# Decoder step on one core: cached latent pages pre-turned by numpy and loaded page by page from SyncE

## The chip, the cores and the metric

The kernel runs on one core of a Trainium2 chip. The metric is device time in microseconds (us) for one launch; runs of one kernel on the same inputs are compared, and the median is quoted. Engines are named as in the profile: PE (TensorE matmul), DVE (VectorE), ACT (ScalarE), POOL (GpSimd), SP (SyncE, which here only issues DMAs).

## The reference, cut to what matters

One inference step of a two-layer trunk: a Mamba-2 SSD layer, then a multi-head latent attention (MLA) layer, for a prompt of 1024 tokens and for 8 sample sequences of 8 new tokens each. The change touches only the sample part of the MLA layer, where the queries attend to 2048 cached tokens per sequence, held in pages of 128 tokens. A page has a latent part (128 x 256) and a rotary part (128 x 32), and `page_table` (8 x 16) says where in the pool each page lies:

```
s = (q_lat . ckv[page_table] + q_pe . kpe[page_table]) * MLA_SCALE      # 128 query rows per sequence
m, l, acc: running maximum, sum of exp, and exp(s - m) @ ckv[page_table]
```

So every latent page is used twice: as keys, with the 256 latent columns on the partitions, and as values, with the tokens on the partitions.

## The kernel before, in words

All matrix products are made of float32 operands split into a high and a low part (`split`: ACT casts the high part, DVE or POOL subtracts for the low part), so one product is three matmuls. The program runs the SSD layer, the MLA projections and gate blocks (about 1010 to 1240 us), sixteen prompt heads (to about 1655), and then the sample attention with the output projection woven into it (1632 to 1915).

The sample attention is the generator `Sample.flow`. It walks over 32 **items**, four for each sequence; an item is four pages, 512 tokens. The order of PE and POOL is as written there (`manual_schedule`); the order of ACT, DVE and SP comes from the framework's scheduler, and each engine runs its own list strictly in order. In step n of the flow:

- `turn(n+1, 0)` and `turn(n+1, 1)` turn the raw page rows of the next item with eight PE transposes (tiles `ct`, four to a PSUM bank) and `split` each bank into `cTh`, `cTl`.
- `turn_p(n-1)` turns the weights of the item before (tile `pt`), which becomes `pTh`, `pTl`.
- `scores(n)` is seven matmuls of 512 columns (tile `sc`); `weigh(n)` is the maximum on DVE and the exp on ACT.
- pieces of the output projection (tile `p`, line 101, twelve matmuls a piece) fill PE, one or two pieces a step from step 9 on. Their result `h` leaves through SP (`out_y_prompt`, line 2016).
- `values(n-1)` is twelve matmuls (tile `o`); `halves(n+1)` splits the raw rows of the next item into `kvh` (ACT) and `kvl` (POOL, four subtractions).
- `load(n+4)` fetches an item: one indirect DMA on POOL's queue, 128 partitions with four token rows of 1 KB each, at addresses from the index tile `ptidx`. Four buffers `pgr` hold raw items (`PRE = 4`). `load_tk` fetches the turned rotary keys of two items at a time, in three DMAs on SP.

The rotary cache is prepared earlier, among the gate blocks: `gather_kpe` collects all 128 rotary pages with one indirect DMA (`kprows`), turns them with 32 PE transposes (`kpt`), splits them (`kpeh`, `kpel`) and writes both to DRAM (`kpe_d`). `page_rows` works out `ptidx` on DVE.

Of the kernel before, what the change touches and what calls it, by code (L numbers as in the profile page):

```python
# [46 lines left out]
SB = {"tr": 4, "sc4": 2, "on": 1, "pj": 1}  # L47
QG = 2
PRE = 4
# [1134 lines left out]
class Heads:  # L1184
# [152 lines left out]
    def load_q(self, pr):  # L1337
        k, nc = self.k, self.k.nc
        qt = self.sp.tile([128, 9, 192], F32, tag="qp", name=f"qp{pr}", bufs=2 if pr else 1)
# [152 lines left out]
def mla_heads(k, hd, sm, early, st):  # L1492
# [46 lines left out]
def gather_kpe(k, pool):  # L1539
    nc, I = k.nc, k.I  # L1540
    idx = pool.tile([128, 1], mybir.dt.int32, name="kpidx")
    nc.sync.dma_start(idx, I["page_table"].rearrange("b (p o) -> (b p) o", o=1))
    rows = pool.tile([NB * NPG, PAGE * ROPE], F32, name="kprows")
    nc.gpsimd.indirect_dma_start(rows, None, I["cache_kpe"].rearrange("o n t c -> (o n) (t c)"),
                                 bass.IndirectOffsetOnAxis(idx, 0), bounds_check=k.npool - 1)
    kh = pool.tile([128, NB * NPG, 32], F32R, name="kpeh")
    kl = pool.tile([128, NB * NPG, 32], F32R, name="kpel")
    rv = rows.rearrange("g (s x) -> g s x", s=32)
    yield
    for g in range(8):  # L1550
        p = k.psum.tile([128, 512], F32, tag="tr", name=f"kpt{g}", bufs=PB["tr"])
        for j in range(4):
            nc.tensor.transpose(p[:, 128 * j : 128 * j + 128], rv[:, 4 * g + j], k.ident)
        split(k, kh[:, :, 4 * g : 4 * g + 4], kl[:, :, 4 * g : 4 * g + 4], p.rearrange("p (s g) -> p g s", s=4))
        yield
    k.kpe_d = []
    for n, t in (("h", kh), ("l", kl)):
        d = k.dram.tile([4, ROPE, NB * NPG * 32], F32, name="kpe_d" + n)
        nc.sync.dma_start(d.rearrange("r c x -> (r c) x"), t.rearrange("p g s -> p (g s)").bitcast(F32))
        k.kpe_d.append(d)  # L1560


def page_rows(k, pool):
    nc, I = k.nc, k.I
    pt = pool.tile([128, NB * NPG], mybir.dt.int32, name="ptab")
    nc.sync.dma_start(pt, I["page_table"].rearrange("b p -> (b p)").partition_broadcast(128))
    ps = pool.tile([128, 1], F32, name="pslot")
    nc.sync.dma_start(ps, I["c_slot"])
    pf = pool.tile([128, 32], F32, name="ptf")
    for j in range(4):  # L1570
        r = slice(32 * j, 32 * j + 32)
        nc.vector.tensor_copy(pf[r], pt[r].rearrange("p (x j) -> p j x", j=4)[:, j])
    nc.vector.tensor_scalar(pf, pf, 32.0, ps, op0=ALU.mult, op1=ALU.add)
    k.ptidx = k.cm.tile([128, 32], mybir.dt.int32, name="ptidx")
    nc.vector.tensor_copy(k.ptidx, pf)


class Sample:
    def __init__(self, k):
        self.k, self.sp = k, None  # L1580
        self.idx = k.ptidx
# [55 lines left out]
    def late_loads(self):  # L1637
        src = self.k.I["mla_w_uv"][0].rearrange("c h v -> c (h v)")
        self.wv = [self.ep.tile([128, D], F32, tag="pgr", name=f"wv4{c}", bufs=4) for c in range(2)]
# [3 lines left out]
    def load_tk(self, n):  # L1643
        k, nc = self.k, self.k.nc
        tk = self.ep.tile([96, 4, 256], F32R, tag="tk", name=f"tk{n}", bufs=2)
        for j in range(3):
            src = k.kpe_d[j % 2][:, :, 128 * n : 128 * n + 256].rearrange("r c x -> c r x")
            with k.tc.issue_after(k.lastq.ins):
                self.lasttk = nc.sync.dma_start(tk[32 * j : 32 * j + 32].bitcast(F32), src)
        for j in range(2):  # L1650
            self.tk[n + j] = tk[:, :, 128 * j : 128 * j + 128]

    def load(self, n):
        k, nc = self.k, self.k.nc
# [61 lines left out]
    def turn(self, n, c):  # L1716
        k, nc, sp = self.k, self.k.nc, self.sp
        raw = self.raw[n]
        pt = self.pt("tr", f"ct{n}_{c}")
        for j in range(4):  # L1720
            nc.tensor.transpose(pt[:, j * 128 : j * 128 + 128], raw[:, j, c * 128 : c * 128 + 128], k.ident)
        th = self.ep.tile([128, 512], F32R, tag=f"cTh{c}", name=f"cTh{n}_{c}", bufs=2)
        tl = self.ep.tile([128, 512], F32R, tag=f"cTl{c}", name=f"cTl{n}_{c}", bufs=2)
        split(k, th, tl, pt)
        self.cT[n, c] = (th, tl)

    def halves(self, n):
        k, nc = self.k, self.k.nc
        raw = self.raw.pop(n)
# [6 lines left out]
    def scores(self, n):  # L1736
# [3 lines left out]
        c0, c1 = self.cT.pop((n, 0)), self.cT.pop((n, 1))  # L1740
        mm3(nc, ps.rearrange("p (r c) -> p r c", r=4), [(x, y if len(y.shape) == 3 else y.rearrange("p (r c) -> p r c", r=4)) for x, y in (
            (k.qlh[:, 0, b], c0[0]), (k.qlh[:, 0, b], c0[1]), (k.qll[:, 0, b], c0[0]),
            (k.qlh[:, 1, b], c1[0]), (k.qlh[:, 1, b], c1[1]), (k.qll[:, 1, b], c1[0]),
            (k.qpr[:, b], self.tk.pop(n)))])
# [67 lines left out]
    def flow(self):  # L1812
        N = len(self.items)
        for n in range(-1, N + 1):
            t, out = n + 1 < N, self.out
            if t:
                self.turn(n + 1, 0)
# [6 lines left out]
            if t:  # L1824
                self.turn(n + 1, 1)
# [16 lines left out]
            if n % 2 == 0 and n + 2 < N:  # L1842
# [283 lines left out]
```

## Time and profile before

| | |
|---|---|
| time, three runs | 1920.44, 1920.27 and 1915.07 us; median 1920.27 |
| profiled execution | span 1915.0 us; no other time is listed for it, and it agrees with the fastest run, 1915.07 |
| busy share of the span | PE 99%, PE weight loads 90%, DVE 63%, ACT 57%, POOL 43% |
| granted PE clock | mean 0.997 of full speed |
| DMA | 212.5 MB, 111 GB/s over the span |
| the 256 transposes `ct` | from 1631.9 to 1870.4 us |
| the 32 transposes `kpt` | from 1069.7 to 1104.5 us |

A busy PE is not PE at its peak, since matmuls overlap in the pipeline. The time that a group of matmuls takes is better read from the distance between starts, or from the chain of work that ended last.

### The profile page before, as it was taken

Reading aid. Unit: us, or ns where it says so; the run is one execution under the profiler, and the core shown is the slowest. Engines: PE = TensorE matmul, PEld = TensorE weight load, DVE = VectorE, ACT = ScalarE, POOL = GpSimd, SP = SyncE. Lnnn points to the kernel's source line nnn. Section 1 sums busy time; section 2 is a strip of 40 time slices with the busy share of each in tenths; the row PEclk is TensorE's granted clock in tenths of the full one; section 3 lists DMA queues with packets and bytes.
Section 4 is the critical chain, followed back from the end, with each engine's and each line's share of the span. In section 5 each row is a group of like instructions: output and inputs, shape, how many; then the busy total and the mean of one; then the engine's idle time right before and its main releaser. Section 6 shows DMA issues by size and latency. Waiting matters only on the chain.

```text
span 1915.0 us, 33672 instructions
## 1 busy us (share of the span) xinstructions
PE 1887.4 (99%) x12023; PEld 1728.1 (90%) x12023; DVE 1208.5 (63%) x2500; ACT 1101.1 (57%) x2528; POOL 823.3 (43%) x1116
## 2 busy tenths in 40 slices
PE   8999999999999999999999999999999999999998
PEld 7999999999999999888788998898888887888887
DVE  5557676757676767765534214566887878666665
ACT  6467666767666666732214323436777777755552
POOL 2447555555655555453004322103443434764551
PEclk9999999999999999999999999999999999999999
DMA  5223323332323232644424662233111112664451
GB/s 165 54 79 91 94 83 94 88 106 83 101 84 99 85 99 78 212 158 175 166 110 133 209 226 75 69 110 95 47 52 41 53 41 58 228 204 142 146 170 37
DMA packets 183967, 212.51 MB, mean 111 GB/s; under 512 B 19148, under 2 KB 147928, under 8 KB 182776
## 3 DMA queue, kind: packets, MB, share of 16 engines
q1 hardware_dynamic: 177304, 185.32, 31.1%
q0 software_dynamic: 6416, 24.91, 3.8%
q8 instruction: 95, 1.56, 0.3%
q14 instruction: 72, 0.59, 0.1%
q10 hardware_dynamic: 80, 0.13, 0.0%
HBM read 151.76 MB, written 58.52 MB: 110 GB/s over the span
## 4 chain that ended last, share of the span: by engine, by line
PE 90%; DMA 3%; DVE 3%; ACT 3%; issue 1%; POOL 0%; SPq 0%; POOLq 0%; DVEq 0%; ACTq 0%
PE pj L89 24%; PE pz L101 8%; PE pq L101 6%; PE pob L101 5%; PE p L101 5%; PE poa L101 4%; PE py L640 3%; PE sc L89 3%; PE o L89 2%; PE sc L1402 2%; PE o L1465 2%; PE o L1467 2%; PE st L1434 2%; PE st L1435 2%; PE st L1436 2%; PE o L1466 2%
## 5 line engine op out<-in xcount | busy, mean ns | idle before, releaser
L89 PE MATMUL pj<-xl,wih 128*128 128x384 f32 (+1 forms) x768 | 255.4, 333 | 0.0
L89 PE MATMUL pj<-xh,wih 128*128 128x384 f32 (+1 forms) x768 | 252.9, 333 | 1.2 <-ACT xh L276 0.8
L89 PE MATMUL pj<-xh,wil 128*128 128x384 f32 (+1 forms) x768 | 252.9, 329 | 0.0
L1448 POOL TENSOR_TENSOR tl<-P,th 128x384 fp32r<-128x384 f32 (+1 forms) x96 | 90.6, 944 | 232.3 <-ACT P L1446 186.6
L528 DVE SCALAR_TENSOR_TENSOR acc<-raw,vec,acc 128x1112 f32<-128x1112 f32 x96 | 141.6, 1476 | 15.3 <-ACT acc L524 14.4
L89 PEld LDWEIGHTS pj<-xh,wih 128*128 128x128 f32 x768 | 143.8, 188 | 2.6 <-ACT xh L276 1.4
L89 PEld LDWEIGHTS pj<-xl,wih 128*128 128x128 f32 x768 | 144.5, 188 | 1.0
L89 PEld LDWEIGHTS pj<-xh,wil 128*128 128x128 f32 x768 | 144.5, 188 | 0.5
L101 PE MATMUL pz<-wih,xh 128*128 128x256 f32 x504 | 143.3, 288 | 1.4 <-ACT z L569 1.4
L101 PE MATMUL pz<-wil,xh 128*128 128x256 f32 (+1 forms) x504 | 139.8, 283 | 0.0
L1445 ACT ACTIVATE th<-st 128x512 fp32r<-128x512 f32 x192 | 94.6, 493 | 66.6 <-PE st L1441 50.9
L101 PE MATMUL pz<-wih,xl 128*128 128x256 f32 x448 | 128.5, 287 | 0.0
L1733 POOL TENSOR_TENSOR kvl<-pgr,kvh 128x256 fp32r<-128x256 f32 x128 | 97.8, 791 | 70.6 <-ACT kvh L1731 70.3
L635 ACT ACTIVATE M<-M,tok 128x128 f32<-128x128 f32 (+1 forms) x288 | 90.4, 386 | 51.4 <-DVE M L631 51.2
L136 DVE TENSOR_TENSOR wil<-wraw,wih 128x512 fp32r<-128x512 f32 x88 | 74.4, 851 | 38.2 <-ACT wih L130 31.7
L101 PEld LDWEIGHTS pz<-wih,xh 128*128 128x128 f32 x504 | 95.9, 190 | 2.3 <-ACT z L569 1.8
L1446 ACT ACTIVATE P<-st 128x512 f32<-128x512 f32 x192 | 93.5, 487 | 0.0
L101 PEld LDWEIGHTS pz<-wil,xh 128*128 128x128 f32 (+1 forms) x504 | 92.8, 184 | 0.1
L101 PE MATMUL p<-w,oh 128*128 128x512 f32 (+3 forms) x304 | 88.8, 386 | 0.6 <-DVE h L1983 0.6
L616 POOL TENSOR_TENSOR xdd<-xsT,tok 128x256 f32<-128x256 f32 x64 | 50.0, 781 | 86.4 <-ACT xsT L602 83.3
L101 PEld LDWEIGHTS pz<-wih,xl 128*128 128x128 f32 x448 | 85.4, 191 | 0.7
L1448 DVE TENSOR_TENSOR tl<-P,th 128x512 fp32r<-128x512 f32 x96 | 72.1, 752 | 18.9 <-ACT P L1446 18.7
(830 smaller groups left out, 6212.5 us busy)
## 6 DMA issues: line engine op xcount, KB each, us to landing
wraw<-in_ssd_w_in SPq DMA_DIRECT2D x92, 256.0 KB
M<-acs_d SPq DMA_DIRECT2D x64, 256.0 KB
s<-in_state_ssm SPq DMA_DIRECT2D x32, 256.0 KB
y_d<-y SPq DMA_DIRECT2D x64, 128.0 KB
out_s_ssm<-s SPq DMA_DIRECT2D x32, 256.0 KB
q_d<-qt SPq DMA_DIRECT2D x32, 192.0 KB
qp<-q_d SPq DMA_DIRECT2D x8, 768.0 KB
wraw<-in_ssd_w_out SPq DMA_DIRECT2D x10, 512.0 KB
```

The costliest lines, as they stand in the source:

```text
L89: nc.tensor.matmul(out, a, b, start=(i == 0), stop=(i == n - 1))
L101: nc.tensor.matmul(o, a, b, start=(j == 0), stop=(j == len(ops) - 1))
L136: return (eng or nc.vector).tensor_tensor(lo, src, hi.bitcast(F32), op=ALU.subtract)
L528: last = nc.vector.scalar_tensor_tensor(acc, raw[:, j : j + n], k.convw[j][:, blk : blk + 1], acc, op0=ALU.mult, op1=ALU.add)
L616: nc.gpsimd.tensor_tensor(v3(xdd), v3(xsT), hb(2), op=ALU.mult)
L635: nc.scalar.activation(M[:m, h, :m], M[:m, h, :m], AF.Exp, bias=tk[:, 0, 4 * g + h : 4 * g + h + 1])
L640: nc.tensor.matmul(py[:m, h * 64 : h * 64 + 64], M[:m, h, :m], xsT[:m, h * 64 : h * 64 + 64], start=True, stop=True)
L1402: nc.tensor.matmul(ps[:, :n], qh[:96, 128 * i : 128 * i + 128], kh[:96, 512 * c : 512 * c + n], start=True, stop=True)
L1445: nc.scalar.activation(th[:, :n], ps[:, :n], AF.Exp, scale=SCALE)
L1446: nc.scalar.activation(P[:, :n], ps[:, :n], AF.Exp, scale=SCALE)
L1448: eng.tensor_tensor(tl[:, :n], P[:, :n], th[:, :n].bitcast(F32), op=ALU.subtract)
L1733: nc.gpsimd.tensor_tensor(rl[:, j], raw[:, j], rh[:, j].bitcast(F32), op=ALU.subtract)
```

## The change

Numpy now builds two arrays on the host. `c_pages` holds for every page 128 rows of 512 numbers: row p is first the 256 latent values of token p, then the two turned halves (latent columns p and 128 + p over the 128 tokens). `c_rope` holds each rotary page already turned. The kernel then does without the transposes `ct` and `kpt`. `load` becomes four plain DMAs on SP, one for each page (256 KB), with the page number read from SBUF into a register; an item is 1 MB in place of 0.5 MB. There are three buffers in place of four. `cast` splits the turned half straight from SBUF: one ACT cast of 1024 columns and two DVE subtractions of 512. `load_tk` fetches one item at a time. The rotary rows are split in SBUF and written to DRAM in runs of 512 bytes. The index arithmetic of `page_rows` is gone. The PSUM banks for turned tiles go from four to three, and those for the output pieces from one to two; the query tiles `qp` move to a pool that is closed at head 14.

```diff
-SB = {"tr": 4, "sc4": 2, "on": 1, "pj": 1}
+SB = {"tr": 3, "sc4": 2, "on": 1, "pj": 2}
-PRE = 4
+PRE = 3
...
-    nc.gpsimd.indirect_dma_start(rows, None, I["cache_kpe"].rearrange("o n t c -> (o n) (t c)"),
-                                 bass.IndirectOffsetOnAxis(idx, 0), bounds_check=k.npool - 1)
+    nc.gpsimd.indirect_dma_start(rows, None, I["c_rope"], bass.IndirectOffsetOnAxis(idx, 0), bounds_check=k.npool - 1)
...
-        p = k.psum.tile([128, 512], F32, tag="tr", name=f"kpt{g}", bufs=PB["tr"])
-        for j in range(4):
-            nc.tensor.transpose(p[:, 128 * j : 128 * j + 128], rv[:, 4 * g + j], k.ident)
-        split(k, kh[:, :, 4 * g : 4 * g + 4], kl[:, :, 4 * g : 4 * g + 4], p.rearrange("p (s g) -> p g s", s=4))
+        c = slice(512 * g, 512 * g + 512)
+        split(k, kh[:, c], kl[:, c], rows[:, c])
...
+            with k.tc.issue_after(k.lastq.ins):
+                self.lasttk = nc.sync.dma_start(tk[32 * j : 32 * j + 32].bitcast(F32),
+                                                k.kpe_d[j % 2][:, 512 * n : 512 * n + 512])
...
-        raw = self.ep.tile([128, 4 * KVL], F32, tag="pgr", name=f"pgr{n}", bufs=4)
-        nc.gpsimd.indirect_dma_start(raw, None, k.I["cache_ckv"].rearrange("o n (s r) c -> (o n s) (r c)", r=4),
-                                     bass.IndirectOffsetOnAxis(self.idx[:, n : n + 1], 0),
-                                     bounds_check=k.npool * 32 - 1)
+        raw = self.ep.tile([128, 4, 512], F32, tag="pgr", name=f"pgr{n}", bufs=PRE)
+        _, pages = nc.values_load_multi_w_load_instructions(
+            k.ptab[0:1, 4 * n : 4 * n + 4], engines=[nc.sync.engine], min_val=0, max_val=k.npool - 1,
+            skip_runtime_bounds_check_because="the DMA that takes the value checks it against the pool's size")
+        for j, pg in enumerate(pages):
+            nc.sync.dma_start(raw[:, j], k.I["c_pages"][bass.ds(pg, 1)].rearrange("o p c -> (o p) c"))
...
-    def turn(self, n, c):
-        k, nc, sp = self.k, self.k.nc, self.sp
-        raw = self.raw[n]
-        pt = self.pt("tr", f"ct{n}_{c}")
-        for j in range(4):
-            nc.tensor.transpose(pt[:, j * 128 : j * 128 + 128], raw[:, j, c * 128 : c * 128 + 128], k.ident)
-        th = self.ep.tile([128, 512], F32R, tag=f"cTh{c}", name=f"cTh{n}_{c}", bufs=2)
-        tl = self.ep.tile([128, 512], F32R, tag=f"cTl{c}", name=f"cTl{n}_{c}", bufs=2)
-        split(k, th, tl, pt)
-        self.cT[n, c] = (th, tl)
+    def cast(self, n):
+        src = self.raw[n][:, :, 256:].rearrange("p g (c t) -> p c g t", c=2)
+        th, tl = (self.ep.tile([128, 2, 4, 128], F32R, tag="cT" + x, name=f"cT{x}{n}", bufs=2) for x in "hl")
+        self.k.nc.scalar.copy(th, src)
+        for c in range(2):
+            self.k.nc.vector.tensor_tensor(tl[:, c], src[:, c], th[:, c].bitcast(F32), op=ALU.subtract)
+        self.cT[n] = [tuple(x[:, c].rearrange("p g t -> p (g t)") for x in (th, tl)) for c in range(2)]
...
-                self.turn(n + 1, 0)
+                self.cast(n + 1)
...
-                self.turn(n + 1, 1)
...
-            if n % 2 == 0 and n + 2 < N:
+            if n >= 0 and n + 2 < N:
                 self.load_tk(n + 2)
```

The first place is PE's list between the values of one item (`o`) and the scores of the next (`sc`), late in the flow. Before:

```order
L89 MATMUL o_22594<-kvh,pTl_22536 128x256
L1721 MATMUL ct_0_22617<-ident,pgr_22369 128x128 [waits DMASW7_49,Activation_49]
L1721 MATMUL ct_0_22617<-ident,pgr_22369 128x128 x3
L1711 MATMUL o46n<-cn_22455,pn_22567 128x256 [waits DMAHW7_49,PE_49]
L1760 MATMUL pt_22630<-ident,P_22560 128x128 [waits PE_49,Activation_49]
L1760 MATMUL pt_22630<-ident,P_22560 128x128 x3
L1721 MATMUL ct_1_22639<-ident,pgr_22369 128x128 [waits DVE_49]
L1721 MATMUL ct_1_22639<-ident,pgr_22369 128x128 x3
L89 MATMUL sc_22648<-cTh_0_22526,qlh 128x512
```

The same place now:

```order
L89 MATMUL o_22925<-kvh,pTl_22866 128x256
L1700 MATMUL o47n<-cn_22775,pn_22888 128x256 [waits DMAHW7_49,Activation_49]
L1745 MATMUL pt_22957<-ident,P_22881 128x128 [waits Activation_49]
L1745 MATMUL pt_22957<-ident,P_22881 128x128 x3
L89 MATMUL sc_22966<-cTh_22855,qlh 128x512
```

The two groups of four transposes are gone; what is left stands in the old order.

The second place is SP's list late in the flow, where an output tile is written (`out_y_prompt`); `[waits ...]` names the engines or DMA semaphores that a row waits for. Before, where the page loads stood on POOL:

```order
L1935 DMA h_21870<-h_d 128x1024 [waits DMAHW0_49]
L1619 DMA cn_22064<-cs_d 8x256 [waits DMAHW1_49,PE_49]
L2016 DMA out_y_prompt<-h_21556 128x512 [waits DMAHW2_49,DVE_49]
L2016 DMA out_y_prompt<-h_21556 128x512 [waits DMAHW3_49,DVE_49]
L1649 DMA tk_21960<-kpe_dh 32x4x256 [waits DMAHW4_49,PE_49]
L1649 DMA tk_21960<-kpe_dl 32x4x256 [waits DMAHW5_49]
L1649 DMA tk_21960<-kpe_dh 32x4x256 [waits DMAHW6_49]
```

Now (`ISA` is an instruction that handles the page number, `TENSOR_LOAD` reads four numbers of `ptab`):

```order
L1637 DMA tk_22517<-kpe_dh 32x512 [waits DMAHW5_49,PE_49]
L2000 DMA out_y_prompt<-h_22134 128x512 [waits DMAHW6_49,DVE_49]
L1637 DMA tk_22517<-kpe_dl 32x512 [waits DMAHW7_49]
L2000 DMA out_y_prompt<-h_22134 128x512 [waits DMAHW0_49,DVE_49]
L1637 DMA tk_22517<-kpe_dh 32x512 [waits DMAHW1_49]
L1643 TENSOR_LOAD ptab
L1647 ISA
L1647 DMA pgr_22503<-in_c_pages 128x512 [waits DMAHW2_49,Activation_49,Pool_49]
L1647 ISA
L1647 DMA pgr_22503<-in_c_pages 128x512 [waits DMAHW3_49]
L1647 ISA
L1647 DMA pgr_22503<-in_c_pages 128x512 [waits DMAHW4_49]
```

A page load now stands behind the output writes, which wait for DVE, and it waits itself for the ACT cast and the POOL subtraction that free its buffer.

The third place is ACT's list among the gate blocks, where the rotary pages are split. Before, spread over five gate blocks, each behind its transposes:

```order
L130 CAST wgh<-wraw 128x1024 [waits DMAHW1_49,Activation_49,Pool_49]
L994 ACTIVATE gt_12864<-pj 128x384 [waits DMAHW3_49,PE_49,Activation_49]
L994 ACTIVATE gt_12864<-pj 128x384 [waits PE_49]
L130 CAST kpeh<-kpt_12943 128x128x4 [waits DVE_49,PE_49]
L130 CAST kpeh<-kpt_12993 128x128x4 [waits PE_49]
L130 CAST kpeh<-kpt_13031 128x128x4 [waits PE_49]
```

Now all eight in one run, ahead of the two gate activations:

```order
L130 CAST wgh<-wraw 128x1024 [waits DMAHW2_49,Activation_49,Pool_49]
L130 CAST kpeh<-kprows 128x512 [waits DMASW2_49,DVE_49]
L130 CAST kpeh<-kprows 128x512 x7
L994 ACTIVATE gt_12854<-pj 128x384 [waits DMAHW2_49,PE_49,Activation_49]
L994 ACTIVATE gt_12854<-pj 128x384 [waits PE_49]
```

The gate activations `gt`, which empty the PSUM tile `pj` for PE, have moved behind the casts.

## Rows read from the trace of the kernel before

**Rows 1.** The page, part 4: the chain that ended last, by engine.

```profile
PE 90%; DMA 3%; DVE 3%; ACT 3%; issue 1%; POOL 0%; SPq 0%; POOLq 0%; DVEq 0%; ACTq 0%
```

**Rows 2.** Windows: busy us by engine, PEclk, DMA share, GB/s.

```profile
1632.00:1700.00 68.00, 64.88 (x392) 55.59 (x391) 44.73 (x92) 48.21 (x105) 46.07 (x55) 0.95 0.75 252
...
1720.00:1840.00 120.00, 120.00 (x716) 103.77 (x716) 78.88 (x175) 65.00 (x141) 63.09 (x77) 1.00 0.49 154
```

**Rows 3.** Chain in order of time, 1741 to 1756: start us, us, what.

```profile
1752.48 0.44 PE ct L1721 x4
1752.92 0.44 PE pt L1760 x4
1753.36 0.44 PE ct L1721 x4
1753.79 1.63 PE sc L89 x7
```

**Rows 4.** Chain: start of the scores of item 7.

```profile
1690.81 1.63 PE sc L89 x7
```

**Rows 5.** Chain: start of the scores of item 31, the last.

```profile
1877.04 1.64 PE sc L89 x7
```

**Rows 6.** PE's timeline at the first rotary transposes.

```profile
1069.83 1.47 PE L1553 MATMUL kpt<-ident,kprows 128*128 128x128 f32 x12
1071.05 0.39 PE L89 MATMUL pj<-hh,wgh 128*128 128x320 f32 x1
```

**Rows 7.** DVE's timeline at 1621.

```profile
1621.05 4.71 DVE L1448 TENSOR_TENSOR tl<-P,th 128x512 fp32r<-128x512 f32 x1
```

**Rows 8.** POOL's timeline at 1618.

```profile
1618.45 1.61 POOL L1656 DMA_INDIRECT pgr<-in_cache_ckv,ptidx  x1 [0.40 <-issue]
```

**Rows 9.** PE's timeline at 1622, with its idle time.

```profile
1622.78 0.50 PE L1467 MATMUL o<-tl,Vh 128*128 128x512 f32 x1 [1.28 <-POOL tl L1448]
...
1625.82 0.50 PE L1467 MATMUL o<-tl,Vh 128*128 128x512 f32 x1 [0.85 <-DVE tl L1448]
```

**Rows 10.** Windows of 5 us, as rows 2.

```profile
1665.00:1670.00 5.00, 4.37 (x25) 3.06 (x23) 3.27 (x6) 4.09 (x11) 3.48 (x5) 1.00 1.03 351
1670.00:1675.00 5.00, 3.45 (x18) 2.87 (x18) 3.83 (x10) 1.96 (x5) 1.03 (x1) 0.82 1.04 377
1675.00:1680.00 5.00, 5.00 (x16) 3.87 (x17) 2.01 (x4) 2.81 (x5) 3.75 (x5) 0.50 0.58 232
```

**Rows 11.** By shape, 1632 to 1915: xcount | busy us, mean ns | idle.

```profile
L1733 POOL TENSOR_TENSOR kvl<-pgr,kvh 128x256 fp32r<-128x256 f32 x128 | 97.8, 791 | 70.6 <-ACT kvh L1731 70.3 <-issue 0.3
...
L136 DVE TENSOR_TENSOR cTl<-ct,cTh 128x512 fp32r<-128x512 f32 x64 | 43.8, 684 | 18.6 <-ACT cTh L130 18.2
...
L1656 POOL DMA_INDIRECT pgr<-in_cache_ckv,ptidx x30 | 31.4, 1048 | 9.5 <-POOL kvl L1733 8.1 <-issue 0.7 <-POOL tl L1448 0.3
```

**Rows 12.** Groups by shape, DVE, whole span.

```profile
L136 DVE TENSOR_TENSOR wil<-wraw,wih 128x512 fp32r<-128x512 f32 x88 | 74.4, 851 | 38.2 <-ACT wih L130 31.7 <-PE pj L89 3.5 <-issue 2.1
```

**Rows 13.** ACT's timeline, 1065 to 1071.

```profile
1065.91 0.49 ACT L994 ACTIVATE gt<-pj 128x384 f32<-128x384 f32 x1 [2.36 <-PE pj L89]
1070.02 0.49 ACT L994 ACTIVATE gt<-pj 128x384 f32<-128x384 f32 x1 [3.62 <-PE pj L89]
1070.46 1.56 ACT L130 CAST kpeh<-kpt 128x512 fp32r<-128x512 f32 x3
```

**Rows 14.** SP's timeline, 1738 to 1747.

```profile
1738.28 0.30 SPq L1649 DMA_DIRECT2D tk<-kpe_dh  x1
...
1739.58 0.43 SPq L1935 DMA_DIRECT2D h<-h_d  x1
...
1745.31 1.49 SPq L2016 DMA_DIRECT2D out_y_prompt<-h  x2
```

**Rows 15.** SP's queue waits, 1700 to 1885: us in total, times, longest.

```profile
SPq L2016 <- DVE h L2014: 37.6, 12, 12.4
```

**Rows 16.** DMA issues: xcount, median us to landing.

```profile
pgr<-in_cache_ckv,ptidx POOLq DMA_INDIRECT x32, 4.6
```

More of the change, by code (lines that the diff above doesn't have):

```diff
@@ L1256, in open @@
         self.add_v(sp, 1)
+        self.rst = ExitStack()
+        self.rows = self.rst.enter_context(open_pool(tc, name="rows3", bufs=1, side="right"))
         self.ogs = [[sp.tile([128, 512], F32, name=f"{n}{q}") for n in ("og", "rl")] for q in range(2)]
@@ L1338, in load_q @@
         k, nc = self.k, self.k.nc
-        qt = self.sp.tile([128, 9, 192], F32, tag="qp", name=f"qp{pr}", bufs=2 if pr else 1)
+        qt = (self.rows if pr else self.sp).tile([128, 9, 192], F32, tag="qp", name=f"qp{pr}", bufs=2 if pr else 1)
         src = k.q_d[:, 192 * pr : 192 * pr + 192]
@@ L1504, in mla_heads @@
             early.close()
+            hd.rst.close()
             hd.rope_queries()
@@ L1543, in gather_kpe @@
     rows = pool.tile([NB * NPG, PAGE * ROPE], F32, name="kprows")
-    nc.gpsimd.indirect_dma_start(rows, None, I["cache_kpe"].rearrange("o n t c -> (o n) (t c)"),
-                                 bass.IndirectOffsetOnAxis(idx, 0), bounds_check=k.npool - 1)
-    kh = pool.tile([128, NB * NPG, 32], F32R, name="kpeh")
-    kl = pool.tile([128, NB * NPG, 32], F32R, name="kpel")
-    rv = rows.rearrange("g (s x) -> g s x", s=32)
+    nc.gpsimd.indirect_dma_start(rows, None, I["c_rope"], bass.IndirectOffsetOnAxis(idx, 0), bounds_check=k.npool - 1)
+    kh = pool.tile([NB * NPG, PAGE * ROPE], F32R, name="kpeh")
+    kl = pool.tile([NB * NPG, PAGE * ROPE], F32R, name="kpel")
     yield
     for g in range(8):
-        p = k.psum.tile([128, 512], F32, tag="tr", name=f"kpt{g}", bufs=PB["tr"])
-        for j in range(4):
-            nc.tensor.transpose(p[:, 128 * j : 128 * j + 128], rv[:, 4 * g + j], k.ident)
-        split(k, kh[:, :, 4 * g : 4 * g + 4], kl[:, :, 4 * g : 4 * g + 4], p.rearrange("p (s g) -> p g s", s=4))
+        c = slice(512 * g, 512 * g + 512)
+        split(k, kh[:, c], kl[:, c], rows[:, c])
         yield
@@ L1557, in gather_kpe, with page_table @@
     for n, t in (("h", kh), ("l", kl)):
[L1558 to L1569, printed above, removed]
-    for j in range(4):
[L1571 to L1575, printed above, removed]
+        d = k.dram.tile([ROPE, NB * NPG, PAGE], F32, name="kpe_d" + n)
+        nc.sync.dma_start(d.rearrange("c g t -> g c t"), t.rearrange("g (c t) -> g c t", c=ROPE).bitcast(F32))
+        k.kpe_d.append(d.rearrange("c g t -> c (g t)"))
+def page_table(k):
+    k.ptab = k.cm.tile([1, NB * NPG], mybir.dt.int32, name="ptab")
+    k.nc.sync.dma_start(k.ptab, k.I["page_table"].rearrange("(o b) p -> o (b p)", o=1))
 class Sample:
@@ L1638, in late_loads @@
         src = self.k.I["mla_w_uv"][0].rearrange("c h v -> c (h v)")
-        self.wv = [self.ep.tile([128, D], F32, tag="pgr", name=f"wv4{c}", bufs=4) for c in range(2)]
+        wv = self.ep.tile([128, 4, 512], F32, tag="pgr", name="wv4", bufs=PRE).rearrange("p (c a) e -> p c (a e)", c=2)
+        self.wv = [wv[:, c] for c in range(2)]
         for c in range(2):
@@ L1714, in first_acc @@
         self.state[b][2] = ac
[L1716 to L1725 removed]
+    def cast(self, n):
[5 more added lines that the diff above has]
+        self.cT[n] = [tuple(x[:, c].rearrange("p g t -> p (g t)") for x in (th, tl)) for c in range(2)]
     def halves(self, n):
         k, nc = self.k, self.k.nc
[L1729 removed]
+        raw = self.raw.pop(n)[:, :, :256]
         rh, rl = (x[:, n % 2].rearrange("p (r c) -> p r c", r=4) for x in (self.k.kvh, self.k.kvl))
@@ L1739, in scores @@
         ps = self.pt("sc4", f"sc4{n}")
[L1740 to L1744, printed above, removed]
+        c0, c1 = self.cT.pop(n)
+        mm3(nc, ps, [(k.qlh[:, 0, b], c0[0]), (k.qlh[:, 0, b], c0[1]), (k.qll[:, 0, b], c0[0]),
+                     (k.qlh[:, 1, b], c1[0]), (k.qlh[:, 1, b], c1[1]), (k.qll[:, 1, b], c1[0]),
+                     (k.qpr[:, b], self.tk.pop(n))])
         self.ps[n] = ps
@@ L2025, in layer_mla @@
     k.og_d = k.dram.tile([8, 128, SEQ], F32, name="og_d")
-    k.npool = k.I["cache_ckv"].shape[1]
+    k.npool = k.I["c_pages"].shape[0]
     with ExitStack() as st:
@@ L2114 @@
     arrays, ins, outs = {}, {}, {}
-    given = {n: np.ascontiguousarray(inputs[n]) for n in _INS}
+    given = {n: np.ascontiguousarray(inputs[n]) for n in _INS if not n.startswith("cache")}
+    ckv, kpe = np.asarray(inputs["cache_ckv"])[0], np.asarray(inputs["cache_kpe"])[0]
+    turned = ckv.reshape(-1, PAGE, 2, 128).transpose(0, 3, 2, 1).reshape(-1, 128, 2 * PAGE)
+    given["c_pages"] = np.ascontiguousarray(np.concatenate([ckv, turned], 2))
+    given["c_rope"] = np.ascontiguousarray(kpe.transpose(0, 2, 1).reshape(-1, ROPE * PAGE))
     given.update(consts())
```

17 lines of the change are left out of this document (6 added, 11 removed).

## The prediction, made blind

> **What bounds the kernel now.** I read the page's chain of waits first: PE holds 90% of it, DMA, DVE and ACT 3% each [rows 1]. So a PE instruction counts in full where PE never waits, and that has to be seen stage by stage. In the windows of the sample attention, late (1720 to 1840) PE is busy 120 of 120 us at full clock, with DVE at 78.88 and DMA at 154 GB/s; early (1632 to 1700) it is busy 64.88 of 68, at a clock of 0.95, with DMA at 252 GB/s [rows 2]. Late it is PE alone that sets the time, early something else takes part. From the chain, item 7's scores start at 1690.81 and item 31's at 1877.04, so a step takes 186.23 / 24 = 7.76 us [rows 4, 5], and the chain shows what one holds: two `ct` groups of 0.44 us each beside `pt` and the scores [rows 3]. Per step the late window gives DVE 78.88 / 120 x 7.76 = 5.1 us, ACT 4.2, POOL 4.1, and 1.2 MB of DMA. There are about 2.7 us of room on the next engine.
>
> **What the change takes off PE.** 64 groups `ct` x 0.44 = 28.2 us; the step goes to 7.76 - 0.88 = 6.88 us. The rotary transposes: twelve rows run until the next `pj` starts 1.22 us later, 0.102 each, 32 of them 3.3 us [rows 6]. POOL's indirect page loads go too; beside one at 1618.45 (1.61 us [rows 8]) a DVE subtraction took 4.71 us [rows 7], and PE stood idle 1.28 and 0.85 us for such subtractions [rows 9], so 2.1 us come back. Sum: 33.6 us.
>
> **What it puts in the way: DMA bytes, early.** An item is 1.05 MB in place of 0.52. Between 1632 and 1700, 252 GB/s x 68 us = 17.1 MB moved [rows 2], and in its worst windows the DMA share is over 1 at 351 and 377 GB/s, which I read as saturated; there PE drops to 4.37 and 3.45 us of 5, and the granted clock to 0.82 and then 0.50 [rows 10]. The stretch holds about nine steps, so nine more halves of an item: 17.1 + 9 x 0.52 = 21.8 MB in 68 - 9 x 0.88 = 60 us is 363 GB/s, as much as the saturated rows moved. If the weights' transfers spread themselves, nothing is lost; if the saturated stretch of 10 us grows by the 4.7 MB, at 364 GB/s 13 us, nearly all becomes loss. Between 0 and 12 I take 6, since the needed rate is at the middle of the two saturated rows and not beyond them. Net 33.6 - 6 = 27.6 us.
>
> **What I cost at nothing, and its cover.** Each `cTl` now reads both inputs from SBUF. The nearest row with two SBUF inputs at the same shape is `wil`, 851 ns [rows 12], against 684 ns [rows 11]: 2 x 0.17 = 0.33 us a step, DVE 5.4 us of 6.88. The upper bound is a whole `kvl` of POOL held against each, 0.79 us [rows 11]: DVE 6.7, still under 6.88 but barely. A rule of the Trainium skill ("SBUF — State Buffer", section "Who interferes with whom") speaks for that bound: a VectorE instruction with two SBUF inputs contends with a GpSimd instruction that reads SBUF, and one waits for the other to end. By that rule up to 64 x 0.79 = 51 us would be added to DVE's work (1.6 a step, which still ends under 6.88); the row of 851 ns bears out only 0.17 apiece. ACT casts the same 1024 columns in one instruction in place of two; POOL loses 1.05 us a step [rows 11]. The eight rotary casts, 0.52 us each [rows 13], now stand together before the gate activations: 4.2 us, where the gate after the first is due 4.1 us later [rows 13]; without the cover of the second `pj` bank PE would lose some 2 us there, once. Index arithmetic, the smaller `tk` transfers and the query pool move no wait that I can see. I give them 0 to 3 us together and take 0.
>
> **SP, a new worker in each step.** Before, an issue cost SP 0.30 to 0.43 us (three `tk` DMAs from 1738.28 to `h` at 1739.58: 0.43 each), and two output writes took 1.49 [rows 14]. After, a step has three `tk` and four pages, 7 x 0.43 = 3.0 us, and a quarter of a tile's reads and writes, (0.43 + 0.43 + 1.49) / 4 = 0.6: 3.6 us. Five instructions have no row: the TENSOR_LOAD and the four ISA. Their bounds are nothing and 1.05 us, POOL's own instruction that makes addresses from a table [rows 11]; being nearest in kind to SP's shortest issue, 0.30, I take 0.25 each, 1.25 us. SP: 4.9 of 6.88 us. At the upper bound it is 8.9. The Trainium skill ("DMA: Bandwidth & Descriptors", section "Latency and other measured facts") gives a floor of about 600 ns for a tensor load; by that figure SP's step would be an estimated 0.35 us longer, and no run so far shows it.
>
> A load of item n+3 is issued when item n has been cast and halved, and is cast two steps later, at best about 10 us on; less an issue of 2 us and a landing of 4.6 (the median of the old load [rows 16]) some 4 us of slack is left. The late rate is 1.2 + 0.5 MB in 6.88 us, 250 GB/s, under the saturated rows.
>
> **The base.** The sum is against the profiled execution, 1915.0 us; no time outside its span is listed, and it agrees with the fastest run (1915.07). It becomes 1887. The median of the runs is 5.2 us above that one, so the same sum makes 1920.27 - 27.6 = 1892.7; I say **1892**.
>
> **Rivals.**
>
> *Early DMA is the bound.* The page loads stand in SP's list among the weight reads of the last head. For it: the two saturated windows with PE idle and the clock fallen [rows 10]. Against it: the demand just fits. Price: the full 12 us of loss, with a clock that stays at its lower level some 5 us more: 1920.3 - 33.6 + 17 = 1904 (1900 to 1910). A rule of the Trainium skill leans the same way: "DMA: Bandwidth & Descriptors", section "SWDGE vs HWDGE vs iDMA", says that software and hardware DMAs feed different queues inside a DMA engine, served in turn, so pages that leave POOL's queue lose a turn of their own; no trace here shows it yet.
>
> *Page loads held behind output writes.* SP waited 37.6 us in 12 waits for DVE before an output write, the longest 12.4 [rows 15]; page loads now queue behind them, with 4 us of slack. If half of that passes to PE, 1892 + 19 = 1911; if all, 1930. Against it: those waits arise because SP was early and had nothing else, and the writes stand where their piece ends.
>
> *More is gained.* The early stalls (68 - 64.88 = 3.1 us idle and about 0.05 x 68 = 3.4 us of clock [rows 2]) vanish, since DVE and POOL are relieved, and nothing is lost: 1920.3 - 33.6 - 6.5 = 1880.
>
> *The other side: SP's issue becomes the bound.* With the five unseen instructions at 1.05 us each, a step is 8.9 us: (8.9 - 7.76) x 32 = 36 us longer, less the 5.4 of the other terms: 1951. It decides from a step of 7.93 us on (there 32 x 0.17 = 5.4), which is unseen instructions of 0.86 us each. Against it: SP's rows with a full DMA behind them are shorter than that.
>
> **How the numbers follow.** Forecast 1892 (own range 1883 to 1900) 0.58; early DMA 0.20; more gain 0.09; output waits 0.07; SP issue 0.06. 0.3% is 5.8 us, about what a measurement here can tell from no change. Faster means under 1914.5: the first three of these, 0.87. The output waits (1911 to 1930) I split into no change, 0.05, and slower, 0.02; with SP's issue, slower is 0.08. To hold eight in ten the range takes the forecast's, the early case and part of the larger gain: 1880 to 1910.
>
> **What would show it.** Right: PE without `ct` and `kpt`, a step from scores to scores of 6.9 us late, no 4.7 us subtraction, DMA near 1 between 1640 and 1690 with PE waiting on it a few us. SP's rows for TENSOR_LOAD and ISA price the unseen five; over 0.86 us each makes me wrong. PE waiting for `cTl` late, with DVE near 100%, would show the shared inputs; `cTh` waiting for page DMAs late, with SP waiting at the output writes, the third case.

## The result, and the profile after

The changed kernel is slower, not faster: 1927.04 us median (1920.03 to 1928.51, five runs) against 1919.32 (1915.07 to 1920.44, five runs), a ratio of 1.0038 with a 95% interval of 1.0020 to 1.0055. Its profiled execution spans 1925.3 us, against 1915.0. Of these 10.3 us, 4.0 lie in the scores of items 8 to 31, 3.6 in the heads, 1.8 between the heads' last scores and item 0's, 1.3 in the gate blocks; the rest nearly cancels. So late the change lost more than the removed transposes gave.

The page's chain by engine, which answers to [rows 1]:

```profile
PE 77%; DMA 7%; issue 5%; ACT 4%; DVE 3%; POOL 3%; SPq 1%; POOLq 0%; DVEq 0%; ACTq 0%
```

The two stretches of [rows 2], in windows with the same columns:

```profile
1632.00:1700.00 68.00, 60.25 (x328) 50.30 (x327) 44.60 (x89) 47.88 (x95) 38.08 (x45) 0.95 0.71 234
1720.00:1840.00 120.00, 110.48 (x586) 92.13 (x584) 77.89 (x170) 63.94 (x125) 49.20 (x64) 0.97 0.68 210
```

PE lost 13 points of the chain, and late it is busy 110.48 of 120 us where it had been busy all the time. The transposes went, and waits took their place. What PE waits for there, 1700 to 1890 (total, times, longest; before, this view of the same stretch has no row):

```profile
PE pt L1745 <- ACT P L1664: 11.3, 10, 3.0
PE o L89 <- DVE pTl L136: 2.4, 3, 1.0
PE sc L89 <- ACT cTh L1708: 1.7, 1, 1.7
```

It waits for the exp (`P`), and hardly for the cast of the turned pages. What ACT itself waits for longest in the same stretch:

```profile
ACT cTh L1708 <- DMA pgr<-in_c_pages: 32.5, 13, 4.4
```

And SP's queue, 1640 to 1890, with the page loads (L1647) and the output writes (L2000):

```profile
SPq L1647 <- POOL kvl L1719: 19.9, 11, 2.9
...
SPq L2000 <- DVE h L1998: 6.8, 9, 1.9
```

The timeline of one step puts the three together: POOL, SP, ACT, DVE and PE in order of time (start, duration, engine, what, and in brackets the idle time before it).

```profile
1855.32 1.97 SPq L1647 DMA_DIRECT2D pgr<-in_c_pages  x4
1856.43 0.48 PE L89 MATMUL sc<-cTh,qlh 128*128 128x512 f32 x1
1859.24 0.21 DVE L1661 TENSOR_SCALAR nm<-mx,nm 128x1 f32<-128x1 f32 x1
1862.29 1.05 ACT L1708 CAST cTh<-pgr 128x1024 fp32r<-128x1024 f32 x1 [4.40 <-DMA pgr<-in_c_pages]
1863.24 0.68 ACT L1664 ACTIVATE P<-sc,nm 128x512 f32<-128x512 f32 x1
...
1864.06 0.66 PE L1745 MATMUL pt<-ident,P 128*128 128x128 f32 x4 [0.84 <-ACT P L1664]
1864.47 0.48 PE L89 MATMUL sc<-cTh,qlh 128*128 128x512 f32 x1
```

The pages issued at 1855.32 are those of item 29; its buffer came free when POOL's last `kvl` of item 26 ended at 1855.29. The scores of item 27 start at 1856.43 and their maximum is ready at 1859.45. The exp could start then, but it starts at 1863.24: the cast of item 29 stands ahead of it in ACT's list and waits 4.40 us for its pages (ACT was ready for it at 1857.89, 2.6 us after the load was issued), although item 29 is not needed on PE until 1873.7. The next scores start 8.04 us after the last.

### The profile page after: what moved, and what is told of

It reads as the page before. It is cut to its first block, busy times and chain, and to the rows that moved or that the text cites. A ratio compares the mean times of both kernels' runs of the same rounds, so it can differ in the third digit from the quotient of the medians.

```text
span 1925.3 us, 33640 instructions
## 1 busy us (share of the span) xinstructions
PE 1872.8 (97%) x11735; PEld 1706.5 (89%) x11735; DVE 1206.2 (63%) x2494; ACT 1097.3 (57%) x2496; POOL 792.9 (41%) x1084
## 4 chain that ended last, share of the span: by engine, by line
PE 77%; DMA 7%; issue 5%; ACT 4%; DVE 3%; POOL 3%; SPq 1%; POOLq 0%; DVEq 0%; ACTq 0%
PE pj L89 21%; PE pz L101 8%; PE pq L101 6%; PE pob L101 5%; PE poa L101 4%; PE py L640 3%; PE p L101 2%; PE sc L1404 2%; PE o L1467 2%; PE st L1436 2%; POOL kvl L1719 2%; PE o L1469 2%; PE st L1437 2%; PE st L1438 2%; PE o L1468 2%
```

## The experiments

The table gives each kernel's median, its ratio to the runs of the kernel before on the same chip (95% interval), and three stretches of its profiled execution, from starts of PE instructions: the gate blocks (first to last `pj<-hh,wgh`), and the scores of item 0 to item 8 and of item 8 to item 31. In before and e5_kpe, where the program of that stretch is the same, single executions read 57.0 and 53.9 us from item 0 to 8, so differences of 3 us say nothing there. The medians of the kernel before differ from chip to chip too, from 1916.8 to 1919.3 us, so a difference of 2 us between two medians of the table is not clear either.

| kernel | median | ratio | gates | items 0–8 | items 8–31 |
|---|---|---|---|---|---|
| before | 1919.3 | | 108.5 | 57.0 | 180.1 |
| changed | 1927.0 | 1.0038 (1.0020–1.0055) | 109.8 | 56.1 | 184.1 |
| e1_pin | 1909.4 | 0.9955 (0.9935–0.9975) | 110.1 | 55.1 | 167.7 |
| e1b_behind | 1914.8 | 0.9976 (0.9962–0.9990) | 112.0 | 51.5 | 175.7 |
| e3_half | 1910.8 | 0.9962 (0.9951–0.9972) | 111.1 | 53.5 | 170.9 |
| e4_noct | 1906.9 | 0.9939 (0.9920–0.9958) | 108.5 | 56.6 | 163.6 |
| e5_kpe | 1916.4 | 0.9997 (0.9986–1.0007) | 111.8 | 53.9 | 180.7 |
| e6_pinhalf | 1910.8 | 0.9973 (0.9960–0.9986) | 111.2 | 55.6 | 163.4 |
| e7_wpool | 1916.7 | 1.0003 (0.9989–1.0017) | 113.5 | 60.6 | 164.7 |
| e8_twice | 1918.6 | 1.0008 (0.9999–1.0017) | 108.5 | 54.9 | 180.1 |
| e9_half4 | 1902.9 | 0.9940 (0.9919–0.9960) | 111.6 | 49.2 | 167.9 |
| e10_nowts | 1905.2 | 0.9944 (0.9927–0.9961) | 111.5 | 52.5 | 163.8 |
| e11_busy | 1910.5 | 0.9966 (0.9955–0.9977) | 110.0 | 56.6 | 165.5 |
| e12_half4pin | 1900.5 | 0.9908 (0.9889–0.9927) | 110.2 | 53.9 | 161.4 |
| e13_rows | 1907.0 | 0.9943 (0.9925–0.9961) | 107.6 | 54.2 | 168.3 |
| e14_pre4 | 1904.6 | 0.9926 (0.9908–0.9945) | 112.3 | 54.2 | 162.5 |
| e15_pre4np | 1908.3 | 0.9949 (0.9930–0.9969) | 110.0 | 51.6 | 168.8 |
| e16_best | 1901.5 | 0.9912 (0.9898–0.9925) | 107.8 | 55.2 | 162.2 |
| e17_qp | 1899.7 | 0.9903 (0.9887–0.9920) | 107.8 | 54.8 | 161.3 |

### Is it ACT's order, or late pages?

The theory after the first look was A: ACT's list is fixed, and a cast that waits for late pages holds up the exp. The rivals were B, the doubled bytes, and C, three buffers whatever the order. **e1_pin** moves the one cast behind the exp:

```diff
-        self.k.nc.scalar.copy(th, src)
+        with self.k.tc.issue_after(self.expi.ins) if n > 1 else nullcontext():
+            self.k.nc.scalar.copy(th, src)
```

> The changed kernel, with the one ACT cast of each item's turned pages held in ACT's list behind the exp of the item two before it (it stood ahead of it). Theory A (ACT's fixed order: the cast waits for pages that land late, and the exp behind it, and with it PE, waits too): the late step falls from 8.0 to 7.0 to 7.4 us, PE's waits for the exp from 11 us to under 4, time 1900 to 1908. Theory B (the doubled bytes are the bound): no change, within 4 us of 1927. Theory C (three buffers make the pages late, whatever the order): PE waits for the cast instead, and the time stays above 1917.

Measured 1909.4, 1.4 us over theory A's range; items 8 to 31 fell from 184.1 to 167.7 us, 7.3 a step, as it said. ACT still waits for pages, but PE hardly waits for the exp, 1700 to 1890:

```profile
ACT cTh L1709 <- DMA pgr<-in_c_pages: 11.2, 7, 4.1
...
PE pt L1746 <- ACT P L1664: 1.7, 2, 1.0
```

**e1b_behind** goes further back: `cast` is called after `turn_p` and held with `issue_after(self.k.cast.ins)`, behind `pTh`.

> The changed kernel, with the cast of an item held in ACT's list behind the cast of the weights of the item two before it (pTh), a place further back than behind the exp. Theory A: the page loads get most of a step more, the late step is 6.9 to 7.1 us and the time 1893 to 1902. Theory B: within 4 us of 1927. Theory C: the cast is then too late for the scores, PE waits for it, and the time is above 1917.

It missed theory A's number: 1914.8, and late PE waits 4.8 us once for the cast and 4.3 us in six waits for the exp. Held that far back, the cast was once late for its own scores. Further back was no better; that it is worse is not clear (the intervals of the two ratios overlap).

**e15_pre4np** leaves the order alone and takes four whole buffers, in the room of one `h5` and one `ol5`; four items are then fetched ahead in place of three (those lines are left out):

```diff
-PRE = 3
+PRE = 4
...
-            h = sp.tile([128, D], F32, tag="h5", name=f"h5{i}", bufs=3)
+            h = sp.tile([128, D], F32, tag="h5", name=f"h5{i}", bufs=2)
...
-            ol = sp.tile([128, 8, 128], F32R, tag="ol5", name=f"ol5{i}", bufs=2)
+            ol = sp.tile([128, 8, 128], F32R, tag="ol5", name=f"ol5{i}", bufs=1)
```

> The same four whole buffers with ACT's order of the changed kernel, the cast not held. If a late page is needed for the blocked exp: ACT's waits for pages fall from 32 us to under 8, steps 8 to 31 take 164 to 168 us, in all 1902 to 1907. If the order alone does it: 175 us or more, above 1912.

The late steps take 168.8 us, about as with the held cast, in the changed kernel's order (both numbers came out a little over the forecast: 168.8 for 164 to 168, 1908.3 for 1902 to 1907). ACT's waits for pages, 1700 to 1890:

```profile
ACT cTh L1708 <- DMA pgr<-in_c_pages: 3.0, 2, 2.4
```

PE has no wait for the exp left there; what it has is 4.4 us in two waits for rotary keys (`tk`). So the loss needs both: the cast ahead of the exp, and pages that come after it. Either cure takes back 15 to 16 of the 20.5 us that lie between 184.1 and the 163.6 of e4_noct below. **e14_pre4** has both cures (the held cast, four whole buffers):

> The kernel with the cast held behind the exp and four whole buffers; the room comes from one buffer fewer of the output's rows (h5) and of its low parts (ol5). If late pages are what holds the first steps: first eight 49 to 52 us, in all 1901 to 1905. If the bytes are: 55 us and 1908. The two buffers taken away may cost PE some us in the later steps.

Late 162.5 us, but the first eight steps did not move (54.2), and its 1904.6 came from the late ones.

### The bytes

**e3_half** loads `c_pages[...][:, 256:]` only.

> The changed kernel, where a page load fetches only the turned half of each row (128 KB in place of 256) and the value rows are split from that half too; the same instructions on every engine. Theory B (bytes): the time falls by 25 us or more, to about 1895 to 1902. Theory A: a load lands about 1 to 1.5 us sooner, of which ACT's 13 late waits take back some 15 us and PE 5 to 12: 1915 to 1922.

Measured 1910.8, between the theories. **e6_pinhalf** is e1_pin with that load.

> The kernel with the cast held behind the exp (1909.4 us) and pages of half the bytes, as in the run with half the bytes. If the doubled bytes cost something of their own once ACT's order is mended: 1900 to 1905, with the first eight steps under 6.5 us. If bytes cost only through the late cast: within 2 us of 1909.

Half the bytes on top of the held cast give nothing in the median (1910.8 and 1909.4): in e3_half they had helped by landing sooner for the cast (ACT's waits for pages 15.0 us, where the changed kernel has 32.5). Late steps are 4 us shorter in the one profile. **e9_half4** and **e12_half4pin** use the room for four half-size buffers, without and with the held cast.

> The changed kernel with pages of half the bytes (values split from the turned half too) and, in the room this frees, four buffers in place of three, so that a load starts a step earlier; ACT's order as in the changed kernel, the cast still ahead of the exp. If the blocked exp takes both, the order and a late page: ACT no longer waits for pages, steps 8 to 31 take 163 to 166 us (184 in the changed kernel, 171 with half the bytes alone), and the time is 1903 to 1908. If the order alone is at fault: 170 us and 1910.

> Half the bytes, four buffers, and the cast held behind the exp. If late pages are all that is left: the first eight steps 49 us and steps 8 to 31 163.5 us, 1895 to 1899. If order and buffers are two cures of one ill: no better than four buffers alone late, 1899 to 1904.

e9_half4 took 1902.9, with one wait of ACT for pages left (3.5 us) and late steps a little over the forecast. In e12_half4pin the cures add 2.4 us in the median, late 161.4, and the 49 us of the first steps in e9_half4 did not repeat. **e7_wpool** is e1_pin with the reads of output weights issued by `nc.gpsimd.dma_start`. They are six in these steps (three of 1 MB, three of 0.5 MB) and not the eight of the text below, and the run also drops the line that held them behind the `tk` loads.

> The kernel with the cast held behind the exp, and the eight reads of output weights (w, w5r) issued from POOL's queue in place of SP's. If SP is held by its own DMAs in flight (an issue waits for the DMA eight issues before it, and a 1 MB read takes 9.5 us): SP's waits for w and w5r vanish, pages come sooner, and the time falls to 1902 to 1907. If only the bytes count: within 3 us of 1909. If POOL's own work is delayed by the issues: slower by up to 8 us.

It was slower than e1_pin by 7 us, and took 60.6 us for the first eight steps. SP's wait for the 1 MB reads (8.2 us in three waits in the changed kernel, 4.7 in e1_pin) is gone there and nothing was gained. What that wait costs by itself is not shown, since the reads also start at other times and POOL has to issue them (0.54 to 0.63 us each).

### What the transposes are worth, and where

**e4_noct** is the kernel before without `ct`:

```diff
-        for j in range(4):
-            nc.tensor.transpose(pt[:, j * 128 : j * 128 + 128], raw[:, j, c * 128 : c * 128 + 128], k.ident)
...
-        split(k, th, tl, pt)
+        split(k, *(x.rearrange("p (r c) -> p r c", r=4) for x in (th, tl)), raw[:, :, c * 128 : c * 128 + 128])
```

> The kernel before, with its 64 groups of transposes left out: the raw rows are cast and subtracted straight from SBUF in their place, so the scores are made of unturned keys; loads, buffers and bytes stay. If the transposes are worth their place on PE (0.44 us a group): 1890 to 1897. If another engine is at once the bound once they go: above 1905. It leaves the rotary part as it was.

It reached 1906.9, 12 us faster and not 28. Late it gained 16.5 us; 22 of the 23 steps from item 8 to 31 held `ct`, so 0.75 a step where I had 0.88, and 1.9 us of new waits of PE for the exp are in it. In the first eight steps it gained nothing, though `ct` took 1.0 us of each. In the profile some is lost ahead of them: from the last head's scores to item 0's it takes 36.5 us, against 30.5, and 3.5 of that is one wait of PE for a head's DMA (`kTh`).

It also shows what moved the cast. In the kernels that keep `ct` (before, e5, e8) the cast of one item beyond stands ahead of each exp in ACT's trace; in e4_noct, where nothing but `ct` went, it is two items nearly throughout, as in the changed kernel. Here the pages were in time: ACT has no wait for them from 1700 to 1890.

**e8_twice** tests the worth of `ct` from the other side (`for j in 2 * list(range(4)) if 1 <= n <= 8 else range(4)`).

> The kernel before, with the transposes of items 1 to 8 made twice into the same tile: 64 more transposes on PE in the first steps of the sample attention, nothing else. If PE is the bound there, 16 groups of 0.44 us: 7 us slower. If something else is the bound there: under 3 us slower, and the first eight steps keep their 7.1 us.

64 more transposes cost 0.08% (-0.01 to 0.17), at most 3.3 us of the 7. The windows from 1660 to 1700 in the kernel before:

```profile
1660.00:1680.00 20.00, 17.82 (x92) 14.49 (x93) 12.32 (x27) 12.03 (x25) 12.14 (x16) 0.83 0.90 315
1680.00:1700.00 20.00, 19.55 (x126) 17.16 (x125) 14.92 (x33) 12.50 (x26) 11.03 (x15) 1.00 0.83 270
```

In e8_twice:

```profile
1660.00:1680.00 20.00, 20.00 (x142) 18.02 (x141) 14.43 (x33) 13.23 (x30) 13.03 (x17) 1.00 0.80 272
1680.00:1700.00 20.00, 20.00 (x139) 18.18 (x138) 14.79 (x34) 13.23 (x28) 13.38 (x18) 1.00 0.97 309
```

The added work filled PE's idle time, and the clock stayed at 1.00 where it had been 0.83. That is the room: the 3.1 us idle and some 3.4 us of clock in [rows 2], 6.5 of the 7 us. So work added to PE has nearly no price there, and the run does not say what PE waits for. **e11_busy** puts such work into e1_pin (eight transposes of `ident` a step), and **e10_nowts** takes the weight reads and their splits out of it.

> The kernel with the cast held behind the exp, and eight transposes of a constant in each of the steps 0 to 7, into a bank that nobody reads: PE gets back as much work as was taken from these steps. If PE's idle time there lowers the granted clock and this costs time: the clock stays at 1.0, the first eight steps fall by 2 to 5 us, 1904 to 1907. If PE's work counts there: 5 us slower, 1914. If neither: within 2 us.

> The kernel with the cast held behind the exp, without the six reads of output weights in the first steps and their three splits (the products take the weights already there). If these reads are what keeps the first eight steps at 55 us once PE has less to do: 46 to 50 us, and 1900 to 1904 in all. If not: 53 to 56 us and within 3 us of 1909.

e11_busy changed nothing (1910.5), though from 1660 to 1700 the clock is 1.00 in its profile and 0.93 and 0.81 in e1_pin's. e10_nowts gained 4 us in its median, some 2 against the kernel before on its own chip; its first steps took 2.6 us less, within their scatter, and missed 46 to 50.

### The rotary part

**e5_kpe** puts the new `gather_kpe`, alone, into the kernel before.

> The kernel before with the rotary part of the change alone: rotary pages turned on the host, split in SBUF, written in 512-byte runs, no 32 transposes; pages, buffers and the 64 groups of transposes as before. If the 32 transposes are worth what they took on PE: 3 us faster, the first head of the prompt starts 3 us earlier. If the eight casts in one run and the short writes give it back: within 1 us, or 1 to 3 us slower.

No gain: 0.9997. The gate blocks, 108.5 us in all three kernels with the old part, take 111.8, with the 32 transposes gone. In its windows PE loses 3.5 us and some clock while DMA is busy (before, PE is busy 20.00 us in both at a clock of 1.00, with 210 and 252 GB/s):

```profile
1070.00:1090.00 20.00, 20.00 (x125) 20.00 (x124) 3.61 (x5) 4.25 (x7) 5.14 (x8) 1.00 0.92 271
1090.00:1110.00 20.00, 16.47 (x88) 15.83 (x88) 6.77 (x5) 5.95 (x11) 10.34 (x14) 0.90 0.80 282
```

**e13_rows** is e1_pin with the two 2 MB writes as whole rows:

```diff
-        d = k.dram.tile([ROPE, NB * NPG, PAGE], F32, name="kpe_d" + n)
-        nc.sync.dma_start(d.rearrange("c g t -> g c t"), t.rearrange("g (c t) -> g c t", c=ROPE).bitcast(F32))
+        d = k.dram.tile([NB * NPG, ROPE * PAGE], F32, name="kpe_d" + n)
+        nc.sync.dma_start(d, t.bitcast(F32))
...
```

> The kernel with the cast held behind the exp, with the split rotary pages written to DRAM as whole rows of 16 KB in place of 512-byte runs (the reads then take 512-byte runs). If the short writes hold up the weight loads that ACT waits for: the gate blocks take 105 to 108.5 us in place of 110 to 112, and the time is 1904 to 1907. If the casts in one run are the cause: no change there.

The gates take 107.6 us, and the same windows show PE at work again:

```profile
1070.00:1090.00 20.00, 20.00 (x124) 20.00 (x123) 7.32 (x8) 5.95 (x12) 8.47 (x10) 1.00 0.76 282
1090.00:1110.00 20.00, 19.72 (x118) 19.41 (x117) 6.45 (x5) 7.73 (x13) 11.68 (x14) 1.00 0.82 285
```

The short writes were the larger part: the three kernels with whole rows take 107.6 to 107.8 us, the thirteen others with the new part 109.8 to 113.5. The eight casts in one run stayed. Without the 32 transposes 105.2 us were to be had (108.5 less 3.3); most of what is missing is a wait of PE for DVE (`hl`, line 277) at about 1041, 1.7 us in e13_rows, 1.4 to 2.0 in every kernel of the changed kind and not there in the kernel before or e5_kpe. It comes ahead of the casts, and its source is open. That ACT's weight casts pass the delay of the writes on is only partly seen: their waits for `w5s` total 5.4 us before, 22.3 in e1_pin and still 17.3 here, but the longest went from 7.5 to 5.5 and PE's wait for `gt` from 2.8 to 0.5.

### The query loads, and all cures together

> Four whole buffers, the cast held behind the exp, and whole-row writes of the rotary pages. If the two add up: gate blocks 107 to 109 us, steps 8 to 31 162 to 165 us, the median 1901 to 1904. If the reads in 512-byte runs make tk late in the steps: 1904 to 1908.

**e16_best** (e14_pre4 with e13_rows) gave 1901.5: they add up. One loss was left in every kernel of the changed kind but e17: the heads (first to last `sc<-kTh,qTh`) take 352 to 354 us, against 350 to 351. In the changed kernel SP issues the second load of queries (`qp`, L1344) between the stores of queries, ACT waits 5.21 us for a store, and PE for ACT (SP, ACT and PE, timeline):

```profile
1294.72 0.39 SPq L1344 DMA_DIRECT2D qp<-q_d  x1
1295.20 0.54 SPq L1180 DMA_DIRECT2D q_d<-qt  x1
...
1300.29 1.05 ACT L1170 COPY qt<-pq 128x384 f32<-128x384 f32 x2 [5.21 <-DMA q_d<-qt]
1300.82 0.69 PE L101 MATMUL pq<-wqh,cqh 128*128 128x384 f32 x1 [2.08 <-ACT qt L1170]
```

The clock was 0.66 from 1300 to 1305. **e17_qp** is e16_best with that load held (`lastqd` is the last write of queries):

```diff
-            nc.sync.dma_start(k.q_d[t0 : t0 + m, cs], qf[:m])
+            k.lastqd = nc.sync.dma_start(k.q_d[t0 : t0 + m, cs], qf[:m])
...
-        with k.tc.issue_after(k.lastq.ins) if pr > 1 else nullcontext():
+        with k.tc.issue_after((k.lastq if pr > 1 else k.lastqd).ins) if pr else nullcontext():
```

> Four whole buffers, held cast, whole-row writes, and the second load of queries held in SP's list behind the last write of queries that is ahead of it in the program, as it stood before the change. If the early load holds up the query writes, ACT's copies and so PE: the wait of 2 us near 1298 goes, the heads take 350 to 351.5 us in place of 354, in all 1898 to 1900. If the wait has another source: 1901.5 within 1.5.

The wait is gone, the heads take 349.7 us, and the median is 1899.7, a ratio of 0.9903: faster than both kernels. Its late window answers to [rows 2]:

```profile
1720.00:1840.00 120.00, 120.00 (x670) 102.02 (x670) 88.76 (x193) 70.34 (x141) 59.59 (x73) 1.00 0.83 245
```

## Why the prediction was wrong, by its steps

**PE as the bound late: right.** Where few or no waits come in, the time follows PE's work (e4_noct, e14_pre4, e17_qp). The size was nearly right too: e17_qp, in whose late steps PE waits for nothing, takes 18.8 us less than the kernel before over the 22 steps that held `ct`, 0.85 a step for the 0.88 forecast.

**The base: probably misread, without harm.** In all runs listed since, the time lies 1.7 us or more above the span, so the execution of 1915.0 us was hardly the fastest run. The forecast was taken from the median and does not hang on it.

**28.2 us for 64 groups: the first step that failed.** I counted the transposes of the early steps at full price, although I had read there that "early something else takes part". Adding work there cost little, taking it away gained nothing. About nine of the 32 steps, 8 us of the sum.

**The load's slack of 4 us: the step that decided the sign.** I had the cast two steps behind the issue, "at best about 10 us on". Issue and landing were right, 6.6 us forecast and 7.0 measured (1855.32 to 1862.29); but ACT was at the cast 2.6 us after the issue, and not 10, and waited 4.40: ACT's list has the cast of item n+2 ahead of the exp of item n. Before, the transposes on PE, whose order is written by hand, kept the cast in its place; without them it depends on nothing but the pages, and the scheduler moved it ahead (e4_noct). Of the order on ACT I had looked at the gate blocks and not at the flow. The price is 20.5 us (184.1 less 163.6), more than the 16.5 that the late steps gained in e4_noct.

**Early DMA, 6 us within 0 to 12: not seen as bytes.** e6_pinhalf against e1_pin is no change.

**The rotary part, 3.3 us: given back.** I had named 2 us that PE would lose without cover, behind the casts; in e5_kpe the loss was as large as the gain, and the larger part of it came from the 512-byte writes, which the sum did not have. In the changed kernel the wait for `hl` at 1041 came on top (1.6 us), a wait that I had not seen either; PE's waits for `gt` behind the casts come to 2.4 us.

**The 2.1 us of stalls: replaced.** Page loads now stand on SP ahead of a head's small DMA: four of them from 1619.19, `qTh` at 1621.19, and PE waits for it:

```profile
1624.35 0.47 PE L1436 MATMUL st<-qTh,kTh 98*128 98x512 f32 x1 [2.33 <-DMA qTh<-nd]
```

**The query pool, "no wait that I can see": 2 to 4 us** (1.8 in the medians of e16_best and e17_qp, 4.3 in their heads), a DMA moved in SP's list that I had not followed.

**SP's issue and DVE: hidden as forecast, the prices lower.** The unseen instructions, by line (min/median/max ns):

```profile
L1643 SPq TENSOR_LOAD <-ptab x32: 296/308/1272, 1613.6 to 1870.7; - x32
L1647 SPq FUSED_REGOPS  x128: 37/37/51, 1614.3 to 1873.0; - x128
L1647 SPq MOVE pgr<-in_c_pages x128: 29/29/38, 1614.3 to 1873.1; - x128
```

One load of four numbers and four pairs is 0.31 + 4 x 0.066 = 0.57 us a step, where I took 1.25. `cTl` from SBUF takes 740 ns:

```profile
L1710 DVE TENSOR_TENSOR cTl<-pgr,cTh 128x512 fp32r<-128x512 f32 x60 | 42.4, 740 | 35.0 <-ACT cTh L1708 28.4 <-DMA tk<-kpe_dh 3.5 <-DMA pgr<-in_c_pages 3.1
```

The Trainium skill ("SBUF — State Buffer", section "Who interferes with whom") would let it wait for a whole `kvl`, 0.79 us. On average here it lost 0.06 against the 684 ns with one input in PSUM; the median is 685 ns and the longest 1769, so a few may have waited like that and most did not, and the measurement decides.

**The rivals.** Page loads held on SP behind output writes (0.07) had the right victim and the wrong place: those writes waited 6.8 us, the page loads 19.9 us for POOL's `kvl`, which frees their buffer, and PE lost through ACT's order. The other side came true by a mechanism that I had not listed.

**Open.** What bounds the first eight steps is not settled. More PE work (e8_twice, e11_busy) cost little or nothing, less (e4_noct) gained nothing; neither half the bytes nor four whole buffers moved them beyond their scatter, nor did leaving out the weight reads. The smaller parts of the change (one PSUM bank fewer for turned tiles, one more for output pieces, the rotary keys fetched item by item, no index arithmetic) were not run by themselves.

## What to carry to other kernels

An instruction that is taken off the path may have been what kept others in order: when it goes, read the list of every in-order engine for what now stands ahead of the critical instruction, and what that waits for. A load that arrives "in time" must be in time for the first instruction queued on it, not for the last one that needs it. And price removed work stage by stage: double it in one stage, and see whether the time moves, with an eye on PE's idle time and clock there, which can swallow what is added.

## What the runs showed of the hardware that was not expected

Writing the same 4 MB to DRAM in runs of 512 bytes rather than of 16 KB cost PE some 2.5 us in the gate blocks (110.1 and 107.6 us), though the rate from 1090 to 1110 was alike (291 GB/s in e1_pin, 285 in e13_rows). When PE paused for about 2 us near 1298, the granted clock went from 1.00 to 0.66 of full speed, a mix of the two levels (1.2 and 2.4 GHz), in the next 5 us: matmuls of 384 columns started 0.32 us apart until 1304.2 and 0.18 before and after, so the wait of 2.08 us cost some 1.4 us more. In e17_qp, without the pause, the clock is 1.00 there. From 1660 to 1680 it is 0.83 in the kernel before, where PE is busy 17.82 of 20 us, and 1.00 in e8_twice, where 64 more transposes keep PE busy throughout.
